# Weight products in unsplit fp32 on the column groups of the array, for a hybrid mLSTM and HGRN2 layer

## The chip, the cores and the metric

The kernel runs on one core of one Trainium2 chip. The core has a matrix engine (TensorE; PE in the profile, its weight loads PEld), a vector engine (VectorE, DVE), a scalar engine (ScalarE, ACT), a general engine (GpSimd, POOL) and an engine that only issues transfers (SyncE, SP). Data lie in an on-chip memory of 128 partitions (SBUF); TensorE writes to eight banks of a second memory (PSUM), from which VectorE and ScalarE take the results. The metric is the device time of the core in microseconds.

## The reference

One layer of a decoder trunk is applied to 320 tokens: a prompt of 256, and eight sequences of eight new tokens with a state each. Everything is in fp32.

```python
D_MODEL, D_FF = 2048, 8192

def layer(x, ...):
    proj = x @ w_in                                 # 2048 x 16392, cut into q, k, v, gates ...
    h, C, n, m = mlstm(q, k, v, ig, lf, C0, n0, m0)     # 4 heads, 256 x 512 state
    branch_a = layernorm(h) * ml_norm_g * sigmoid(ml_o)
    o, S = hgrn2(hq, log(f), 1 - f, hi, S0)             # 8 heads, 128 x 256 state
    branch_b = rms(o) * hg_norm_g * silu(hg_g)
    merged = sigmoid(gate_a) * (branch_a @ w_branch_a) + sigmoid(gate_b) * (branch_b @ w_branch_b)
    x1 = layernorm(ALPHA * x + merged @ w_out)
    hid = square(relu(x1 @ w_up))
    return layernorm(ALPHA * x1 + hid @ w_down), C, n, m, S
```

The outputs are the new rows and the new states of both mixers, for the prompt and for each of the eight sequences.

## The kernel before

**Layout.** Activations lie transposed: 16 blocks of 128 channels on the partitions, with the 320 tokens as columns. All weight matrices are cut into 304 tiles of 2048 inputs by 128 outputs (`tile_list`), taken in a fixed order: the mLSTM heads (v, k, q, with some merge gates between), the HGRN2 heads, the output gates, the two branch projections, the output projection, and four rounds of `up` and `dn` of 16 tiles each. A tile comes in two units of 1024 inputs, 512 KB each, and is summed over 16 steps of k in one PSUM bank. The first three tiles (`FIRST`) come with x itself and make up the lead.

**The product.** TensorE gets no plain fp32 operands in the weight loop. Each operand is split into a high part, rounded to the type `float32r`, and a low part, the rounded rest. A step of k is three matmuls of a 128 x 128 weight block and 128 x 320 tokens: high by high, high by low, low by high. In `run_main`:

```python
self.mm(o, hi[:, kk], mh[:, k, :], start=k == 0, stop=False)
self.mm(o, hi[:, kk], ml[:, k, :], start=False, stop=False)
self.mm(o, lo[:, kk], mh[:, k, :], start=False, stop=k == KT - 1)
s.t["pe"] = max(s.t["pe"], at) + 441.0
```

The weights are split on the chip: `prep` takes a unit out of one of three raw buffers `wr`, lets ScalarE write the high part (`wh`, in later stages a part of `bb`) and VectorE the low part (`wl` or `bb`), and then has the raw buffer loaded again (`reload`, on SP's queue). The operands x, the two branches, the merged branches, the normalised x1 and the hidden rows are split in the same way as they are made (`split`), into pairs such as `xh` and `xl`, `bah` and `bal`, `bbh` and `bbl`. The attention products of both mixers are partly split (numerator, final state, HGRN2 output, the sums over ones) and partly plain fp32 matmuls (scores, row sums).

**Small products on parts of the array.** Three kinds of matmul use only some columns or rows of the array: the projection for the two mLSTM gates at the end of `lead` (16 matmuls, L768 to L770), whose 32 outputs go to the four 32-wide column groups in turn; the product of the sample queries with their states (`m_sample`, `h_state`), eight matmuls of 32 outputs in a block; and the updates of the sample states (`m_adds`, `h_update`), four matmuls of 32 rows in a block. The first two are plain fp32.

**Order.** One Python program writes the instructions of all engines in the order of a plan. The class `Sched` keeps a planned time for each engine; `run_main` writes the steps of the weight loop one by one, and after each one `pump` lets the chains of small work (evacuations, the two mixers, LayerNorm, transfers) write what they can by the plan. The plan takes its durations from formulas: `pe_r` for a rounded matmul, `pe_f` for an fp32 one, `act` and `dve` for the other engines, 441 ns for a step of the weight loop. Each engine then runs its own instructions in that order and waits on semaphores; the plan's times themselves are not in the program. Transfers are issued by SP in one queue, some of them ("lazy") only when the plan has few bytes under way. Three PSUM banks serve the weight tiles, more from the output gates and the output projection on, and the others the small products.

**Ends.** After the last `dn` tile come the last LayerNorm, its scaling of all 16 blocks on VectorE and ScalarE with the stores of y, and, on TensorE between them, the final states of the prompt: `m_C` (16 products of 128 x 512 over three matmuls each) and `h_S` (16 fp32 matmuls of 128 x 256). Their operands were put into DRAM by the mixers (`kD`, `vD`, `sD`, `iD`).

Of the kernel before, what the change touches and what calls it, by code (L numbers as in the profile page):

```python
# [21 lines left out]
KT = 16  # L22
# [51 lines left out]
FIRST = 3  # L74
# [212 lines left out]
def pe_r(n):  # L287
    return max(108.0, n * 0.425)
# [44 lines left out]
class Program:  # L333
    def __init__(self, tc, nc, d, pools):
# [7 lines left out]
        self.xh2 = p.tile([128, KT, TOK + 2], F32R, name="xh", tag="xh")  # L342
        self.xl2 = p.tile([128, KT, TOK + 2], F32R, name="xl", tag="xl")
        self.xh, self.xl = self.xh2[:, :, 0:TOK], self.xl2[:, :, 0:TOK]
        self.RAW, self.HL = 3, 3
# [8 lines left out]
        self.ra = p.tile([128, 6656], F32R, name="ra", tag="ra")  # L354
# [21 lines left out]

    def dma(self, out, in_):
        self.nc.sync.dma_start(out, in_)
        self.s.transfer(self.s.t["sp"], 4 * math.prod(out.shape), 4 * min(run(out), run(in_)))


    def carve(self):
# [13 lines left out]
        A, B, C, R = Part(self.f1), Part(self.f2), Part(self.f3), Part(self.ra[:, 0:6400])  # L396
# [3 lines left out]
        self.vt = Pool([Part(self.f1, 4608).three(3, 512)])  # L400
# [3 lines left out]
        self.kw = Pool([B.three(2, 320)])  # L404
# [13 lines left out]
        self.shl = Pool([(R(384), R(384), R(256))])  # L418
        self.vhl = Pool([R(2048).rearrange("p (x s v) -> p x s v", x=2, s=2)])
        self.vs = Pool([R(512)])  # L420
        self.khl = Pool([R(1024).rearrange("p (x s k) -> p x s k", x=2, s=2)])
# [3 lines left out]
        A, B, R = Part(self.f1, 6144), Part(self.f2), Part(self.rh)  # L425
# [9 lines left out]
        self.hkz0 = self.ra[:, 5376:6400]  # L435
        self.phl = Pool([self.ra[:, 3776:5376].rearrange("p (x c) -> p x c", x=2)])
        self.hkst = Pool([self.hkz0[:, 0:256].rearrange("p (g k) -> p g k", g=2)])
# [11 lines left out]
    def carve_h(self):  # L449
# [7 lines left out]
        rxb = self.pool.tile([128, 4096], F32R, name="rxb", tag="rx")  # L457
        X, R, V, W, Z = self.Part(rxb), self.Part(self.ra), self.Part(self.ra), self.Part(rxb, 2880), self.Part(rxb, 3840)
        self.nc.gpsimd.memset(rxb[:, 3840:4096].bitcast(F32), 0.0)
        self.halves = Pool([(V(512), V(512), W(448), W(448))])  # L460
        self.vp = Pool([V(256), rxb[:, 2624:2880]])
        self.ats = Pool([(Z(128), Z(128))])
        self.bah = Slices([(X if j < 12 else R)(TOK) for j in range(KT)])
        self.bal = Slices([R(TOK) for _ in range(KT)])
# [13 lines left out]
    def carve_x(self):  # L478

        self.sx = []  # L480
        for name, n in (("xh", 6), ("xl", 2)):
            R = self.Part(self.pool.tile([128, KT * (TOK + 2)], F32, name=name + "s", tag=name))
            self.sx += [R(768) for _ in range(n)]

    def carve_o(self):
        R = self.Part(self.pool.tile([128, 4096], F32, name="oC", tag="rx"))
        self.oC = [R.three(2, 512) for _ in range(MH)]
        self.oS = self.Part(self.pool.tile([128, 6656], F32, name="oS", tag="ra")).three(HH, 256)

    def carve_b(self):  # L490

        self.bb = self.pool.tile([128, 10240], F32R, name="bb", tag="f1")
        R = self.Part(self.bb)
        self.bbh, self.bbl = R.three(KT, TOK), R.three(KT, TOK)
        R = self.Part(self.bb)
        wide = [R(2048) for _ in range(5)]
        self.wx = [(w[:, 0:1024], w[:, 1024:2048]) for w in wide]
        self.wxv = [w.rearrange("p (x s v) -> p x s v", x=2, s=2) for w in wide]


    def prep(self, must=False):

        u = self.next_prep
        if u >= len(UNITS) or not self.hl_free:
            return False
        now = self.s.t["pe"]
        if must:
            self.s.until(lambda: u in self.raw_at)
        elif u not in self.raw_at:
            return False  # L510
        if not must and (self.raw_at[u] > now + 200 or self.hl_free[0][0] > now + 200 or self.s.t["dve"] > now + 1200):
            return False
        at, buf = self.hl_free.pop(0)
        raw = self.wr[:, u % self.RAW, :]
        hi, lo = buf
        s = self.s
        e = s.use("act", max(at, self.raw_at[u]) + LAT, act(1048))
        self.A(hi, raw)
        e = s.use("dve", e + LAT, dve(1034))
        self.V().tensor_tensor(lo, raw, hi.bitcast(F32), ALU.subtract)  # L520
        self.unit[u] = (buf, e + LAT)
        self.next_prep += 1
        if u + self.RAW < len(UNITS):
            s.spawn(self.reload(u + self.RAW, e), -1)
        return True

    def reload(self, u, at):
        t = yield ("sp", 620, lambda: self.dma(self.wr[:, u % self.RAW, :], self.d["wt"][u]), (at,))
        self.raw_at[u] = t

    def run_main(self):
# [3 lines left out]
        for n in range(len(UNITS) * 8):  # L535
# [4 lines left out]
            if k == 0:  # L540
                self.before(i, t)
                mh, ml, evs = self.moving(t)
                todo[i] = self.take(), mh, ml, evs
            b, mh, ml, evs = todo[i]
            o = b[:, :mh.shape[2]]
            while self.prep(u not in self.unit):
                pass
            assert u in self.unit, (u, self.next_prep)
            (hi, lo), at = self.unit[u]
# [3 lines left out]
            kk = slice(128 * (k % 8), 128 * (k % 8) + 128)  # L553
            self.mm(o, hi[:, kk], mh[:, k, :], start=k == 0, stop=False)
            self.mm(o, hi[:, kk], ml[:, k, :], start=False, stop=False)
            self.mm(o, lo[:, kk], mh[:, k, :], start=False, stop=k == KT - 1)
            s.t["pe"] = max(s.t["pe"], at) + 441.0
            if k % 8 == 7:
                self.give(u)
# [4 lines left out]
        self.carve_o()  # L564
# [11 lines left out]
    def give(self, u):  # L576

        now, hl = self.s.t["pe"], self.unit[u][0]
        wide = any(hl is w for w in self.wx)
        rest = self.next_prep >= len(UNITS)  # L580
        if u + 16 < len(UNITS) or not (rest or (self.n_vx < 3 if wide else self.n_kx < 1)):
            self.hl_free.append((now, hl))
        elif wide:
            self.n_vx += 1
            self.vx.free.append((now, self.wxv[[hl is w for w in self.wx].index(True)]))
        else:
            self.n_kx += 1
            self.kx.free += [(now, x.rearrange("p (x s k) -> p x s k", x=2, s=2)) for x in hl]


    def moving(self, t):
        kind = t[0]
        if kind == "wa":
            return self.bah, self.bal, self.ba_ev
        if kind == "wb":
            return self.bbh, self.bbl, self.bb_ev
        if kind == "wo":
            return self.bah, self.bal, self.mg_ev
        if kind == "up":
            return (self.xh, self.xl, self.xs_ev) if t[2] else (self.xh2, self.xl2, self.zg_ev)  # L600
        if kind == "dn":
            return self.bah, self.bal, self.hid_ev[t[2]]
        return self.xh, self.xl, None

    def before(self, i, t):
# [29 lines left out]
        elif kind == "wo" and h == 0:  # L635
# [3 lines left out]
            self.hl_free += [(s.t["pe"], x) for x in self.wx[:4]]  # L639
            R = self.Part(self.wxv[4].rearrange("p x s v -> p (x s v)"))  # L640
            self.lns = [R.three(2, TOK) for _ in range(3)]
# [3 lines left out]
        elif kind == "dn" and c == 0 and h == 0:  # L645
            s.spawn(self.xs_(), 0)
        elif i == len(TILES) - 8:
# [10 lines left out]
    def start(self):  # L658
# [11 lines left out]
        self.unit, self.raw_at, self.next_prep = {}, {}, 0  # L670
# [12 lines left out]
        for u in range(self.RAW):  # L683
            self.dma(self.wr[:, u, :], d["wt"][u])
            self.raw_at[u] = 19000.0 + 1500.0 * u
        self.dma(self.cst, d["cst"])
        self.dma(self.f2[:, 448:704], d["spread"])
        self.spread = self.ra[:, 6400:6656].rearrange("p (g n) -> p g n", g=2)
# [7 lines left out]
        self.hl_free, self.gw = [], gw  # L696
        for e in s.t:
            s.t[e] = 2000.0
        s.wire, s.lands = 22000.0, [22000.0] * 8
# [24 lines left out]
    def lead(self):  # L724

        s, v = self.s, self.nc.vector
        f = lambda x: x.bitcast(F32)
        flat = lambda x: x.rearrange("p a b -> p (a b)")
        wh, wl = flat(self.wh), flat(self.wl)
# [4 lines left out]

        def halves(x, h, l, n, at):
            e = s.use("act", at + LAT, act(n))
            self.A(h, x)
# [1468 lines left out]
```

## Time and profile before

| | us |
|---|---|
| median of three runs | 2277.47 |
| lowest and highest of them | 2276.78, 2277.49 |
| span of the profiled execution, first to last instruction | 2275.6 |
| TensorE busy, in the profile | 2267.5 |
| VectorE busy | 1392.1 |
| ScalarE busy | 1170.8 |

The profile page has, from the top: busy time by engine; the span in 40 slices, with the granted clock of TensorE and the traffic; the transfer queues; the chain of work that ended last; the costliest groups of instructions, by source line, engine, operation and operands, with count, busy time, mean duration and the idle time before them; and the transfers. Because nearly every matmul is recorded by one helper, all have the line L375; ScalarE's have L369 and SP's transfers L378. In a row such as `bank<-xh,wl 128*128 128x320 f32`, the operands are followed by the rows and columns of the array that are used and by the shape of the streamed operand. Matmuls overlap in the pipeline and the profile's durations hold its depth, so the pace of a stream is read from starts, or from a stretch's length and its count, not from the duration of one.

### The profile page before, as it was taken

To read this page: it belongs to the slowest core of one execution; us is meant where nothing else is said; L and a number is where in the kernel's file an instruction comes from. 1 tells how busy PE (TensorE), PEld (TensorE's weight loads), DVE (VectorE), ACT (ScalarE), POOL (GpSimd) and SP (SyncE) were. 2 spreads that over 40 slices of the span, in tenths; PEclk is the share of its full clock that TensorE was granted. 3 is DMA by queue.
4 is the path that set the end of the run, shared out by engine and by line. 5 is a ranking of instruction groups with operands and counts; after the bars stand their busy time and mean duration, and the time that the engine had idled before them with its cause. 6 is when DMAs were issued, how large, how long until landed. Compare 5 with 4: busy or idle time off the path is not lost.

```text
span 2275.6 us, 39057 instructions
## 1 busy us (share of the span) xinstructions
PE 2267.5 (100%) x15518; PEld 2230.4 (98%) x15518; DVE 1392.1 (61%) x2426; ACT 1170.8 (51%) x2081; POOL 12.5 (1%) x36
## 2 busy tenths in 40 slices
PE   9999999999999999999999999999999999999998
PEld 9999999999999999999999999999999999999998
DVE  5676777777777777666555767544444444444456
ACT  6566555678777766444433446533432343234334
POOL 0000000000000000000000000000000000000000
PEclk9999999999999999999999999999999999999999
DMA  7588898666666575555556544444444444444476
GB/s 283 175 266 253 277 285 248 211 191 189 188 195 211 178 216 175 175 173 172 172 173 198 193 153 147 148 150 151 153 148 148 149 151 153 150 148 148 150 229 194
DMA packets 227438, 424.95 MB, mean 187 GB/s; under 512 B 96436, under 2 KB 122932, under 8 KB 226232
## 3 DMA queue, kind: packets, MB, share of 16 engines
q1 hardware_dynamic: 222376, 415.98, 56.9%
q0 software_dynamic: 4736, 6.29, 1.2%
q8 instruction: 121, 1.98, 0.4%
q14 instruction: 61, 0.50, 0.1%
q10 hardware_dynamic: 144, 0.20, 0.0%
HBM read 371.49 MB, written 50.90 MB: 186 GB/s over the span
## 4 chain that ended last, share of the span: by engine, by line
PE 97%; ACT 2%; DVE 0%; issue 0%; ACTq 0%; POOL 0%; DVEq 0%; POOLq 0%
PE bank L375 97%; ACT f L369 1%; ACT wh L369 0%; ACT f3m L369 0%; ACT ra L369 0%; ACT oC L369 0%; DVE f3m L2090 0%; DVE f3m L2097 0%; DVE wl L520 0%; ACT oS L369 0%; ACT xh L369 0%; ACTq L2202 0%; ACT f3h L369 0%; DVE f L1975 0%; DVE f L1974 0%
## 5 line engine op out<-in xcount | busy, mean ns | idle before, releaser
L520 DVE TENSOR_TENSOR wl<-wr,wh 128x1024 fp32r<-128x1024 f32 x440 | 538.8, 1225 | 432.3 <-ACT wh L369 429.2
L375 PE MATMUL bank<-xh,wh 128*128 128x320 f32 (+1 forms) x2504 | 786.5, 315 | 0.0
L375 PE MATMUL bank<-xh,wl 128*128 128x320 f32 (+1 forms) x2504 | 774.4, 310 | 0.0
L375 PE MATMUL bank<-xl,wh 128*128 128x320 f32 (+1 forms) x2504 | 772.1, 309 | 0.0
L369 ACT ACTIVATE wh<-wr 128x1024 fp32r<-128x1024 f32 x440 | 465.4, 1058 | 456.1 <-PE bank L375 437.0
L375 PEld LDWEIGHTS bank<-xh,wh 128*128 128x128 f32 x2504 | 471.2, 188 | 9.2 <-issue 7.3
L375 PEld LDWEIGHTS bank<-xl,wh 128*128 128x128 f32 x2504 | 471.3, 188 | 3.0
L375 PEld LDWEIGHTS bank<-xh,wl 128*128 128x128 f32 x2504 | 471.6, 188 | 0.2 <-DVE wl L520 0.2
L369 ACT ACTIVATE bb<-wr 128x1024 fp32r<-128x1024 f32 x162 | 171.6, 1059 | 296.0 <-PE bank L375 276.0
L520 DVE TENSOR_TENSOR bb<-wr,bb 128x1024 fp32r<-128x1024 f32 x162 | 198.5, 1225 | 195.2 <-ACT bb L369 195.0
L375 PE MATMUL bank<-ra,wh 128*128 128x320 f32 x1008 | 276.2, 309 | 0.7 <-DVE ra L1778 0.7
L375 PE MATMUL bank<-ra,bb 128*128 128x320 f32 x1096 | 255.5, 309 | 0.0
L375 PE MATMUL bank<-xh,bb 128*128 128x320 f32 (+1 forms) x1136 | 253.8, 309 | 0.0
L375 PE MATMUL bank<-rxb,bb 128*128 128x320 f32 x1088 | 249.1, 309 | 0.0
L375 PEld LDWEIGHTS bank<-xh,bb 128*128 128x128 f32 x1136 | 191.0, 188 | 0.0
L375 PE MATMUL bank<-rxb,wl 128*128 128x320 f32 x608 | 187.9, 309 | 0.0
L375 PE MATMUL bank<-rxb,wh 128*128 128x320 f32 x608 | 187.9, 309 | 0.0
L375 PEld LDWEIGHTS bank<-ra,bb 128*128 128x128 f32 x1096 | 185.2, 188 | 0.0
L375 PEld LDWEIGHTS bank<-rxb,bb 128*128 128x128 f32 x1088 | 184.6, 188 | 0.0
L375 PEld LDWEIGHTS bank<-ra,wh 128*128 128x128 f32 x1008 | 181.3, 188 | 0.9 <-DVE ra L1778 0.9
L375 PE MATMUL bank<-xl,bb 128*128 128x320 f32 (+1 forms) x568 | 175.5, 309 | 0.0
L369 ACT ACTIVATE f<-f 32x128 f32<-32x128 f32 (+6 forms) x405 | 150.7, 373 | 37.1 <-DVE f L1343 19.0
(274 smaller groups left out, 2257.3 us busy)
## 6 DMA issues: line engine op xcount, KB each, us to landing
wr<-wt SPq DMA_DIRECT2D x602, 512.0 KB, 3.4
rx<-C SPq DMA_DIRECT2D x36, 256.0 KB, 5.1
Cs<-rx SPq DMA_DIRECT2D x36, 256.0 KB, 4.5
f<-C SPq DMA_DIRECT2D x28, 256.0 KB, 4.7
Cs<-f SPq DMA_DIRECT2D x28, 256.0 KB, 5.5
f<-first SPq DMA_DIRECT2D x6, 704.0 KB, 9.6
vD<-ra SPq DMA_DIRECT2D x4, 1024.0 KB, 6.5
f<-S SPq DMA_DIRECT2D x8, 512.0 KB, 5.1
```

The source lines that it names most:

```text
L369: return self.nc.scalar.activation(out, in_, func, **kw)
L375: self.nc.tensor.matmul(*a, **kw)
L520: self.V().tensor_tensor(lo, raw, hi.bitcast(F32), ALU.subtract)
```

## The change

All weight products take plain fp32 operands, each as four matmuls of 32 outputs, one for each column group of the array, with the same streamed operand:

```diff
+    def mm4(self, out, w, x, start=True, stop=True, **kw):
+        for a in range(4):
+            c = slice(32 * a, 32 * a + 32)
+            self.nc.tensor.matmul(out[c], w[:, c], x, start=start, stop=stop, **kw)
...
-            (hi, lo), at = self.unit[u]
+            s.until(lambda: u in self.unit)
+            w, at = self.unit[u]
...
-            kk = slice(128 * (k % 8), 128 * (k % 8) + 128)
-            self.mm(o, hi[:, kk], mh[:, k, :], start=k == 0, stop=False)
-            self.mm(o, hi[:, kk], ml[:, k, :], start=False, stop=False)
-            self.mm(o, lo[:, kk], mh[:, k, :], start=False, stop=k == KT - 1)
-            s.t["pe"] = max(s.t["pe"], at) + 441.0
+            self.mm4(b[:, :x.shape[2]], w[:, 128 * (k % 8):128 * (k % 8) + 128], x[:, k, :], k == 0, k == KT - 1)
+            s.t["pe"] = max(s.t["pe"], at) + pe_4(x.shape[2])
```

The splits of weights and operands go, and with them `prep`, `reload` and `split`. The operands are written once, in fp32, into `x`, `ba` and `bb`. The room of the halves goes to raw weight buffers: ten from the start (`RAW`), four more once `bb` is laid out; `give` has a freed buffer loaded with the next unit at once.

```diff
-FIRST = 3
+FIRST, RAW = 3, 10
...
 def pe_r(n):
-    return max(108.0, n * 0.425)
+    return max(108.0, n * 0.425) + 120.0
+
+
+def pe_4(n):
+    return max(60.0, n * 0.84)
...
-        self.xh2 = p.tile([128, KT, TOK + 2], F32R, name="xh", tag="xh")
-        self.xl2 = p.tile([128, KT, TOK + 2], F32R, name="xl", tag="xl")
...
-        self.wr = p.tile([128, self.RAW, 1024], F32, name="wr")
-        self.wh = p.tile([128, self.HL, 1024], F32R, name="wh")
-        self.wl = p.tile([128, self.HL, 1024], F32R, name="wl")
+        self.x2 = p.tile([128, KT, TOK + 2], F32, name="x", tag="x")
+        self.x = self.x2[:, :, 0:TOK]
+        self.ba = p.tile([128, KT, TOK], F32, name="ba")
+        self.wr = p.tile([128, RAW, 1024], F32, name="wr")
...
+    def load(self, u, buf, at):
+        t = yield ("sp", 620, lambda: self.dma(buf, self.d["wt"][u]), (at,))
+        self.unit[u] = (buf, t)
```

`pe_4` is the plan's time for the four matmuls of an `mm4` together; it replaces the 441 ns of a step and `pe_f`. The same `mm4` takes the place of the split products of the mixers, of the plain fp32 products on the whole array, and of the sums over ones in LayerNorm and in HGRN2. The mLSTM numerator and the LayerNorm totals:

```diff
-                for x, w in ((sh, vh), (sh, vl), (sl, vh)):
-                    st, sp = n == 0, n == 3 * len(jobs) - 1
-                    yield ("pe", pe_r(512), lambda: self.mm(b, x[:, c:c + 128], w[:, s, :], start=st, stop=sp))
-                    n += 1
+            for n, (c, s) in enumerate(jobs):
+                yield ("pe", pe_4(512), lambda: self.mm4(b, E[:, c:c + 128], vt[:, s, :], n == 0, n == len(jobs) - 1))
...
-        yield from self.split(x, hi, lo)
-        for i, y in enumerate((hi, lo)):
-            yield ("pe", 147, lambda: self.mm(p[:, :TOK], self.ones.bitcast(F32R), y, start=i == 0, stop=stop and i == 1))
+        yield ("pe", pe_4(TOK), lambda: self.mm4(p[:, :TOK], self.ones, x, start, stop))
```

The spread of the sample rows and the row-tiled updates of the sample states stay as rounded products, each with its split. `kD` and `vD` hold fp32 instead of two halves, are half as large, and are loaded by SP during the second `up` round (`m_load`) instead of by POOL near the end.

More of the change, by code (lines that the diff above doesn't have):

```diff
@@ L456, in carve_h @@
             self.nc.gpsimd.memset(x, 0.0)
[L457 to L464, printed above, removed]
+        X = self.Part(self.pool.tile([128, 4096], F32, name="rxh", tag="rx"))
+        ats = [X(128) for _ in range(2)]
+        for x in ats:
+            self.nc.gpsimd.memset(x, 0.0)
+        self.ats = Pool(ats)
+        self.pb.free.append((self.s.t["pe"], X(800)))
         now = self.s.t["pe"]
@@ L480, in carve_x, with carve_b @@
         self.sx = []
-        for name, n in (("xh", 6), ("xl", 2)):
-            R = self.Part(self.pool.tile([128, KT * (TOK + 2)], F32, name=name + "s", tag=name))
+        for tag, size, n in (("x", KT * (TOK + 2), 6), ("fv", 2176, 2)):
+            R = self.Part(self.pool.tile([128, size], F32, name=tag + "s", tag=tag))
             self.sx += [R(768) for _ in range(n)]
-    def carve_o(self):
+    def carve_b(self):
+        bb = self.pool.tile([128, 10240], F32, name="bb", tag="f1")
+        self.bb = self.Part(bb).three(KT, TOK)
+        self.give([bb[:, lo:lo + 1024] for lo in range(6144, 10240, 1024)])
+        R = self.Part(bb)
+        self.ck = [(R(512), R.three(2, 512)) for _ in range(MH)]
@@ L501, in prep @@
[L501 to L525, printed above, removed]
@@ L541, in run_main @@
                 self.before(i, t)
[L542 to L548, printed above, removed]
-            (hi, lo), at = self.unit[u]
+                x, evs = self.moving(t)
+                todo[i] = self.take(), x, evs
+            b, x, evs = todo[i]
+            s.until(lambda: u in self.unit)
+            w, at = self.unit[u]
+            at += LAT
             if evs is not None:
@@ L574, in take @@
         return b
[L576 to L588, printed above, removed]
     def moving(self, t):
@@ L646, in before @@
             s.spawn(self.xs_(), 0)
+        elif kind == "up" and c == 1 and h == 0:
+            self.ck_ev = [Ev() for _ in range(MH)]
+            for j in range(MH):
+                s.spawn(self.m_load(j), 3)
         elif i == len(TILES) - 8:
@@ L682, in start @@
         self.dma(self.vec, d["vec"])
-        for u in range(self.RAW):
+        for u in range(RAW):
             self.dma(self.wr[:, u, :], d["wt"][u])
[L685 to L688, printed above, removed]
+            self.unit[u] = self.wr[:, u, :], 19000.0 + 1300.0 * u
+            if u == 1:
+                self.dma(self.cst, d["cst"])
+                self.dma(self.f2[:, 448:704], d["spread"])
         nc.gpsimd.memset(self.eps, EPS)
@@ L817, in rows @@
         p1 = yield acq(self.sbank)
-        yield ("pe", pe_f(T), lambda: self.mm(p1[:, :T], sel, gs, start=True, stop=True))
+        yield ("pe", pe_4(T), lambda: self.mm4(p1[:, :T], sel, gs))
         yield rel(self.sbank, b)
@@ L1251, in m_sample @@
         yield rel(self.bc, bc)
-        yield wait(m["KS"])
+        yield wait(m["KS"], m["CP"])
         yield post(m["end"])
@@ L1684, in h_S @@
         b = yield acq(self.mbank)
-        yield ("pe", 2 * pe_f(256), lambda: [self.mm(
-            b[:, 0:256], x[:, 128 * i:128 * i + 128], x[:, 256 + 256 * i:512 + 256 * i], start=i == 0, stop=i == 1) for i in range(2)])
+        yield ("pe", 2 * pe_4(256), lambda: [self.mm4(
+            b[:, 0:256], x[:, 128 * i:128 * i + 128], x[:, 256 + 256 * i:512 + 256 * i], i == 0, i == 1) for i in range(2)])
         self.s.spawn(self.S_out(h, b), 0, self.s.t["pe"])
```

315 lines of the change are left out of this document (104 added, 211 removed).

## The prediction

> **What bounds the kernel now.** I read the head of the page first, then its chain of waits, then the view of stretches for two long pure stretches of the weight loop.
>
> ```profile
> span 2275.6 us, 39057 instructions
> PE 2267.5 (100%) x15518; PEld 2230.4 (98%) x15518; DVE 1392.1 (61%) x2426; ACT 1170.8 (51%) x2081; POOL 12.5 (1%) x36
> PEclk9999999999999999999999999999999999999999
> PE 97%; ACT 2%; DVE 0%; issue 0%; ACTq 0%; POOL 0%; DVEq 0%; POOLq 0%
> 1100.00:1466.00 366.00, 366.00 (x2487) 365.74 (x2487) 232.60 (x344) 172.57 (x252) 0.00 (x0) 1.00 0.52 171
> 1700.00:2250.00 550.00, 550.00 (x3754) 550.00 (x3753) 256.90 (x312) 194.06 (x233) 5.34 (x7) 1.00 0.49 156
> ```
>
> TensorE is busy at full clock for the whole span, the chain that ended last is TensorE for 97%, and the DMA engines are busy 52% and 49% in the two stretches (the number before the last). So the time is the sum of the matmuls, and nothing else needs a price until that sum falls. The last two rows give the unit of the sum: 550 us for 3754 matmuls is 0.1465 us each, 366 for 2487 (some evacuation products among them) 0.1472. A step of k in the weight loop is three of these (high by high, high by low, low by high), so 0.4395 to 0.4415 us; I take 0.440. There are 304 tiles of 16 steps, 4864 steps, 48 of them in the lead.
>
> **What the change puts in its place** is in the trace of before already. The gate projection at the end of `lead` (L768 to L770) is 16 unsplit fp32 matmuls of 128 rows, 32 outputs and 320 tokens, written to the four column groups in turn: the very shape and order of `mm4`. These are the PE rows of the timeline around it, then two groups of the page and of the view by line and shape.
>
> ```profile
> 26.96 0.31 PE L375 MATMUL bank<-xh,wl 128*128 128x320 f32 x1
> 27.19 1.82 PE L375 MATMUL bank<-f,f 128*32 128x320 f32 x24
> 28.83 0.72 PE L375 MATMUL bank<-f 128*32 128x320 f32 x8
> 29.48 0.42 PE L375 MATMUL bank<-xh,wh 128*128 128x320 f32 x1
> 27.49 0.72 PE L375 MATMUL bank<-f,f 128*32 128x320 f32 x8
> 27.19:29.37 2.18, 2.18 (x33) 0.94 (x32) 0.65 (x1) 2.18 (x4) 0.20 (x1) 1.00 0.00 0
> L375 PE MATMUL bank<-ones 128*128 128x128 f32 x18 | 4.2, 430 | 1.0 <-POOL ones L666 1.0
> L375 PE MATMUL bank<-rx,f 128*32 128x512 f32 x72 | 13.6, 599 | 0.0
> L375 PE MATMUL bank<-f 128*32 128x512 f32 x56 | 12.6, 597 | 0.0
> L375 PE MATMUL bank<-ra 128*128 128x512 f32 x52 | 20.2, 395 | 0.0
> ```
>
> Count first. Sixteen calls left 24 + 8 = 32 records; the 64 sample products on column groups left 72 + 56 = 128; the nine warm-up matmuls of ones left 18; the 52 rounded products of this width (9 and 2 and 2 for each of four heads) left 52. An fp32 matmul is two instructions on the array, a rounded one is one. Then the pace. The 32 records run in eight rounds, the four groups of a round side by side (a narrow window at 27.9 shows 8 records from 27.49 on, two rounds overlapping). The second round starts at 27.49 and the seventh at 28.83: five rounds in 1.34 us, 0.268 each; with the first, which follows the change of tile shape, six in 1.64, 0.273. The whole block is 2.18 us for four steps of four, 0.545. I take 0.269 a round, nearer to the undisturbed ones. The four groups do share the time of one, but each of them has two rounds to run, so a step of `mm4` at 320 columns is 2 x 0.269 = **0.538 us, against 0.440** for the three rounded products.
>
> **The sum.** Weight loop: 4864 x (0.538 - 0.440) = +477 us. With the ends of the rows, 0.536 - 0.4415 to 0.546 - 0.4395, it is +460 to +518.
>
> The smaller products. Two widths have rows, from the last stretch of the timeline and from the sample block of a head:
>
> ```profile
> 2260.43 0.84 PE L375 MATMUL bank<-bb,wh 128*128 128x512 f32 x3
> 2261.11 1.52 PE L375 MATMUL bank<-bb,wl 128*128 128x512 f32 x6
> 2262.48 5.34 PE L375 MATMUL bank<-xhs 128*128 128x256 f32 x24
> 104.98 1.48 PE L375 MATMUL bank<-f 128*32 128x512 f32 x10
> 106.30 0.60 PE L375 MATMUL bank<-f 128*32 128x512 f32 x2
> 106.84 0.50 PE L375 MATMUL bank<-ra 32*128 32x512 f32 x4
> ```
>
> Nine rounded products of 512 take 2.05 us, 0.228 each. Column-group rounds of 512 start at 104.98 and, three rounds later, at 106.30: 0.44, the first one again the long one; I use 0.43, so 0.86 for a group of four. Between 320 and 512 I read both on a straight line (an estimate): 256 costs 0.119 rounded and 0.43 for a group, 480 costs 0.214 and 0.81. Then: 12 products of the mLSTM numerator and 16 of its final state, three rounded for one group, 28 x (0.86 - 0.68) = 5; the sample numerator, 4 x (0.86 - 0.46) = 2; the lag sums over ones, 8 x (0.81 + 0.54 - 0.43 - 0.29) = 5; the HGRN output, 8 x (1.29 - 1.07) + 8 x (0.43 - 0.24) = 3; six LayerNorm totals, 6 x (0.54 - 0.29) = 2. Together +17 us. Of this, the 16 final-state products (3 us) lie behind the last tile, where the rows above show TensorE dense from product to product, so they count too. The scores and other products that were fp32 on the whole array already (0.55 us at 320 columns, below) keep their time: bounds 0 to +30 for all of this.
>
> Changes of tile shape. The waits view has the price of all of them now:
>
> ```profile
> PEld bank L375 <- issue: 24.1, 79, 0.8
> L520 DVE TENSOR_TENSOR wl<-wr,wh 128x1024 fp32r<-128x1024 f32 x440 | 538.8, 1225 | 432.3 <-ACT wh L369 429.2
> L369 ACT ACTIVATE wh<-wr 128x1024 fp32r<-128x1024 f32 x440 | 465.4, 1058 | 456.1 <-PE bank L375 437.0
> L375 PEld LDWEIGHTS bank<-xl,wh 128*128 128x128 f32 x2504 | 471.3, 188 | 3.0
> wr<-wt SPq DMA_DIRECT2D x602, 512.0 KB, 3.4
> ```
>
> 79 gaps, 24.1 us. The blocks on column groups (one gate block, eight for mLSTM samples, eight for HGRN) cease to be changes; the row-tiled state products (16 and 8 blocks) still are, and the twelve to sixteen spread blocks and the transposes, which stay on the whole array, become ones. About as many as before: 0, bounds -24 to +24.
>
> What is taken from VectorE and ScalarE (all 602 unit splits; the two rows above are 440 of them, the others write `bb`) is off the path: both engines waited for TensorE or for each other over 430 us in just these groups. It hides behind the matmuls now and its removal buys nothing; the plain copies that remain are shorter than what they replace. The 602 weight loads on SP's queue are the same ones, now into ten, later fourteen, buffers; a unit lasts eight steps, 4.3 us instead of 3.5, against 3.4 us from issue to landing, so the transfers move from half busy to less. The wait of the loop changes its object: a unit's first matmul waits for the landing of its transfer instead of VectorE's low half. All of TensorE stands behind such a wait, but ten units are loaded ahead, 43 us of work. The eight reloads for the final mLSTM state go from POOL's queue to SP's, at the second `up` block, half as large as now and long before they are needed. The program order was made with a faster TensorE in mind (`pe_4` counts 0.84 ns a column, one round where the rows show two). An engine that is slower than its plan finds its inputs ready; what waits is ACT's and VectorE's evacuations, which have 8.6 us a tile. I price it at nothing. LDWEIGHTS of 32 columns sit inside the rounds in the block above (32 in 0.94 us of 2.18), so they add nothing either.
>
> The lead. It starts without the split, so about 1 us sooner, and one of its early waits for the splits goes too; it stays TensorE-bound since three groups are 1.6 us a step: -2, bounds -4 to +3.
>
> Sum against the profiled execution: 2275.6 + 477 + 17 - 2 = 2767.6. The median of the runs shown, 2277.47, is 1.9 above that span, so **2769.5 us**. All ends added, 2277.5 + 460 - 24 - 4 = 2709.5 and 2277.5 + 518 + 30 + 24 + 3 = 2852.5; they will not all fall one way, and 2715 to 2850 is the forecast's own range.
>
> **Rivals.**
>
> One round instead of two (faster). If the array got through a group's fp32 product in a single round of 0.269, as `pe_4` assumes, a step would cost 0.269 and the loop would lose 4864 x 0.171 = 832 us: TensorE 2277 - 832 - some 20 for the small products that shorten too, 1430. Then the transfers take over:
>
> ```profile
> q1 hardware_dynamic: 222376, 415.98, 56.9%
> GB/s 283 175 266 253 277 285 248 211 191 189 188 195 211 178 216 175 175 173 172 172 173 198 193 153 147 148 150 151 153 148 148 149 151 153 150 148 148 150 229 194
> ```
>
> 416 MB at the best slice, 285 GB/s, are 1460 us, so about 1500. It decides from a step under 0.440. For it speaks only that four groups start within one round; against it the count, two records to a call, in all 16 calls here and all 64 sample products. The Trainium skill, TensorEngine Tiling (Array Packing), section Theoretical Speedup, gives up to four-fold where a dimension is 32 or less; set against the 0.55 us of a whole-array fp32 product, that would be 0.14 us a step. The rows bear it out only for four 32-wide products against one 32-wide product, not against a 128-wide one. 8%.
>
> Instruction supply (slower still). A step becomes 8 matmuls and 8 weight loads instead of 3 and 3. From 33.6 ns an instruction on (0.538 / 16) the sequencer would set the pace. The block above issued 64 in 2.18 us, 34 ns each, without a gap, and the next one started after the usual pause; but no longer run of this density is in the trace, and the loop itself shows only that 73 ns each is sustained (550 us for 7507). So the price lies between nothing and 16 x 73 = 1.17 us a step, +3070 us on the forecast, 5840. I take nothing, as the dense block is the nearest row. The Trainium skill, TensorE: Matmul & The Clock Gate, Part 2, step 2, says that with hardware decode off a MATMUL costs the sequencer about 62 ns. By it alone eight take 0.50 us, still under 0.538; with the loads at the same price a step is 0.99 us and the time near 4970. No row here tells which decode is on. 7%.
>
> The four do not run side by side, but as one whole-array fp32 product:
>
> ```profile
> 2251.15 0.71 PE L375 MATMUL bank<-f3m,ones 128*128 128x320 f32 x2
> 2251.70 0.72 PE L375 MATMUL bank<-f,ones 128*128 128x320 f32 x2
> ```
>
> 0.55 us a step, +58 on the forecast, 2830: it is inside the range, and I count it there, with 3%.
>
> **Chances and range.** The forecast with its own range has 80%, the whole-array case 3%, one round 8%, supply 7%, and 2% stay for what I do not see (half of them near no change). About 0.2% is what a measurement of this kernel can tell from no change. Faster: 8%. Same: 1%. Slower: 91%. The range 2715 to 2850 holds 83%; neither far case has to be reached.
>
> **What would show it.** Right: in the page after, PE still 99% or more of the span and near 97% of the chain; some 39,000 matmul records of 128*32 with 320 columns; in a stretch of the loop eight matmuls every 0.538 us; the DMA share below 0.45 there; VectorE's and ScalarE's busy time down by more than 600 us each. Wrong on the fast side: four records to a step, a DMA share near 0.9. Wrong on the supply side: weight loads with idle time before them put down to issue, and rounds further apart than 0.27 us. Wrong on my zero for the order: PE idle behind evacuations at the tile borders.

## The result, and the profile after

| | us | ratio to before |
|---|---|---|
| before, median of 4 runs | 2277.36 | |
| after, median of 4 runs (2803.37 to 2804.77) | 2804.15 | 1.2313 (95%: 1.2296 to 1.2331) |
| forecast | 2769.5 (2715 to 2850) | |

The kernel became 526.8 us slower. The sign, the rough size and the range were right; the forecast was 34.7 us too low. The page of after, head, slices and chain:

```profile
span 2801.9 us, 87737 instructions
PE 2772.6 (99%) x41048; PEld 1587.7 (57%) x41048; DVE 585.6 (21%) x1584; ACT 473.3 (17%) x1281; POOL 7.6 (0%) x31
PE   9999999889999999999999999999999999999998
PEclk9999999989999999999999999999999999999999
PE 98%; ACT 1%; DVE 1%; DMA 0%; issue 0%; ACTq 0%; POOL 0%; DVEq 0%; POOLq 0%
...
wr<-wt SPq DMA_DIRECT2D x494, 512.0 KB, 3.4
```

VectorE lost 806.5 us of work and ScalarE 697.5, and neither is seen in the time: TensorE is busy 99% of the span and 98% of the chain. But the eighth and the ninth slice show 8 for TensorE, and the ninth shows 8 for its clock, where before had nines. The view of stretches of after, first that region as a whole, then the part of it that is starved, then two pure stretches of the weight loop (busy us of PE, weight loads, VectorE, ScalarE, GpSimd; granted clock; DMA share; GB/s):

```profile
500.00:800.00 300.00, 280.41 (x4078) 131.44 (x4074) 125.41 (x413) 131.84 (x427) 3.23 (x11) 0.95 0.54 165
546.10:585.30 39.20, 21.52 (x122) 5.78 (x112) 23.40 (x62) 17.65 (x48) 0.00 (x0) 0.74 0.46 141
1100.00:1466.00 366.00, 366.00 (x5442) 251.58 (x5436) 64.75 (x156) 28.73 (x54) 0.00 (x0) 1.00 0.45 148
2000.00:2400.00 400.00, 400.00 (x5948) 240.06 (x5942) 23.00 (x47) 12.24 (x26) 0.00 (x0) 1.00 0.38 124
```

The last row is the step: 400 us for 5948 matmuls, eight to a step, 0.538 us, the forecast's figure to the third digit. The second row is what the forecast did not have: 39 us in which TensorE ran 122 matmuls, against some 580 in such a time in the loop. TensorE's timeline there, with its idle time and what ended it in brackets:

```profile
539.75 6.38 PE L382 MATMUL bank<-x,wr 128*32 128x320 f32 x92
545.94 0.35 PE L382 MATMUL bank<-misc,f 128*32 128x1 f32 x24
556.09 0.79 PE L377 MATMUL bank<-ra 128*128 128x512 f32 x1 [9.80 <-DVE ra L911]
556.81 1.94 PE L382 MATMUL bank<-fv,f 128*32 128x512 f32 x8
...
567.24 3.64 PE L382 MATMUL bank<-fv,f 128*32 128x512 f32 x16 [1.80 <-DVE rx L1209]
...
574.67 1.89 PE L377 MATMUL bank<-rx,f 128*32 128x512 f32 x4 [1.45 <-DMA rx<-C]
...
576.92 1.07 PE L382 MATMUL bank<-fv,f 128*32 128x512 f32 x8
...
583.09 2.23 PE L377 MATMUL bank<-ra 32*128 32x512 f32 x3 [2.28 <-DVE f L1209]
585.25 5.04 PE L382 MATMUL bank<-x,wr 128*32 128x320 f32 x44
```

The rows that multiply by a weight buffer, `bank<-x,wr`, stop at 546 and come back at 585.25. Between them stands nothing but the last mLSTM head's small products, one behind the other, with waits for VectorE, for ScalarE and, in one row, for a transfer. In the longest gap, 9.8 us, ScalarE writes that head's values block by block. This is ScalarE's timeline of after:

```profile
549.95 4.24 ACT L371 ACTIVATE fv<-f 32x256 f32<-32x256 f32 x11
```

To see where the difference lies, I added up the starts of all matmul records: the lead up to the first step behind the gate block, the steps of the weight loop (from a step's record to the next record), the blocks of other matmuls between them, and the tail from the last weight record to the end of the span. What lies between a step and a block beside it is counted in the record that comes first. Two experiments told of below are in the table too (the slower plan, and whole-array products in the loop).

| us | before | after | slower plan | whole-array loop |
|---|---|---|---|---|
| lead | 29.5 | 33.3 | 33.7 | 34.0 |
| weight steps | 2138.9 | 2603.0 | 2599.0 | 2629.9 |
| blocks between | 81.8 | 134.8 | 104.1 | 157.9 |
| tail | 25.4 | 30.8 | 25.9 | 30.9 |
| span | 2275.6 | 2801.9 | 2762.7 | 2852.7 |

### The profile page after: what moved, and what is told of

It is laid out like the page before. It is cut to its first block, busy times and chain, and to the rows that moved or that the text cites. A ratio compares the mean times of both kernels' runs of the same rounds, so it can differ in the third digit from the quotient of the medians.

```text
span 2801.9 us, 87737 instructions
## 1 busy us (share of the span) xinstructions
PE 2772.6 (99%) x41048; PEld 1587.7 (57%) x41048; DVE 585.6 (21%) x1584; ACT 473.3 (17%) x1281; POOL 7.6 (0%) x31
## 3 DMA queue, kind: packets, MB, share of 16 engines
q1 hardware_dynamic: 216872, 415.98, 46.6%
## 4 chain that ended last, share of the span: by engine, by line
PE 98%; ACT 1%; DVE 1%; DMA 0%; issue 0%; ACTq 0%; POOL 0%; DVEq 0%; POOLq 0%
PE bank L382 97%; PE bank L377 2%; ACT f L371 0%; ACT fv L371 0%; ACT ra L371 0%; DMA Cs<-f 0%; DVE f3m L1958 0%; DMA hH<-f 0%; ACT f3m L371 0%; DVE f3m L1951 0%; DVE oS L1588 0%; DVE f L1209 0%; DVE f L1023 0%; DVE f L989 0%; ACT misc L371 0%
## 5 line engine op out<-in xcount | busy, mean ns | idle before, releaser
L382 PE MATMUL bank<-x,wr 128*32 128x320 f32 (+1 forms) x21248 | 1474.0, 433 | 0.0
L382 PEld LDWEIGHTS bank<-x,wr 128*32 128x32 f32 x21248 | 761.9, 109 | 639.0 <-issue 39.4
L382 PE MATMUL bank<-ba,wr 128*32 128x320 f32 x8960 | 609.7, 432 | 0.0
L382 PEld LDWEIGHTS bank<-ba,wr 128*32 128x32 f32 x8960 | 376.7, 110 | 226.2
L382 PE MATMUL bank<-ba,bb 128*32 128x320 f32 x3328 | 227.8, 432 | 0.0
L382 PE MATMUL bank<-x,bb 128*32 128x320 f32 (+1 forms) x2944 | 201.7, 432 | 0.0
L382 PEld LDWEIGHTS bank<-ba,bb 128*32 128x32 f32 x3328 | 140.7, 110 | 83.3
L382 PEld LDWEIGHTS bank<-x,bb 128*32 128x32 f32 x2944 | 124.2, 109 | 74.3 <-issue 2.0
L382 PE MATMUL bank<-bb,wr 128*32 128x320 f32 x1408 | 95.5, 432 | 0.0
L371 ACT ACTIVATE f<-f,misc 128x320 f32<-128x320 f32 x162 | 90.8, 560 | 18.1 <-DVE f L1916 10.2
L382 PEld LDWEIGHTS bank<-bb,wr 128*32 128x32 f32 x1408 | 67.2, 110 | 27.6
L382 PE MATMUL bank<-bb 128*32 128x320 f32 (+1 forms) x768 | 57.9, 459 | 0.0
L382 PEld LDWEIGHTS bank<-bb 128*32 128x32 f32 x768 | 34.6, 110 | 21.6 <-issue 8.6
L382 PE MATMUL bank<-f 128*32 128x320 f32 (+4 forms) x768 | 43.8, 345 | 0.0
```

What stands on the lines that cost most here:

```text
L371: return self.nc.scalar.activation(out, in_, func, **kw)
L382: self.nc.tensor.matmul(out[c], w[:, c], x, start=start, stop=stop, **kw)
```

## The experiments

Theory: a step costs 2 rounds of 0.269 us, the four groups side by side, and the missing 35 us come from the order that the plan wrote with half of TensorE's real time. Rivals: the missing time lies in the column groups themselves or in changes of tile shape; and the two far rivals of the prediction, one round and instruction supply.

**A plan with TensorE's real time.** `pe_4` and the gate block are doubled in the plan. The work of the engines stays the same, only its order changes.

```diff
-    return max(60.0, n * 0.84)
+    return max(120.0, n * 1.68)
...
-        s.t["pe"] += 1100.0
+        s.t["pe"] += 2200.0
```

> The changed kernel, with the plan told what the loop takes: pe_4 1.68 ns a column with a floor of 120 instead of 0.84 and 60, 2200 instead of 1100 for the gate block. The instructions are the same, only their order differs. In the changed kernel's trace TensorE lacks weight steps from 546.1 to 585.3 us, a stretch of 39 us with some 10 us of small products in it. Theory A: the order was made for a TensorE of half the pace, whose plan ran out of weight steps at the first HGRN2 tiles; a right plan puts weight steps between the last mLSTM products, the stretch closes, and the time is 2804 - 29 = 2775 (2765 to 2785). Rival: the last mLSTM head ends late because of its new buffers and chains, whatever the plan; then the stretch stays and the time is 2798 to 2810.

Measured: 2765.15 us (2764.70 to 2765.59, 4 runs), 1.2141 of before (1.2123 to 1.2159), 39.0 us less than after. The head of its page and its stretches:

```profile
span 2762.7 us, 87781 instructions
PE 2758.0 (100%) x41048; PEld 1632.1 (59%) x41048; DVE 608.2 (22%) x1584; ACT 475.6 (17%) x1281; POOL 7.6 (0%) x31
```

```profile
500.00:800.00 300.00, 300.00 (x4628) 146.94 (x4624) 123.98 (x383) 124.35 (x405) 1.82 (x5) 1.00 0.51 162
1000.00:2700.00 1700.00, 1700.00 (x25240) 1112.64 (x25236) 223.48 (x497) 120.94 (x255) 0.00 (x0) 1.00 0.40 134
```

The same 41,048 matmuls, and the stretch from 500 to 800 us has 300 busy of 300, where after had 280. The timeline of this kernel's TensorE shows how: at the same time it is already at the small products of an HGRN2 head, and weight steps stand between them.

```profile
548.27 0.40 PE L382 MATMUL bank<-f,f3h 128*32 128x128 f32 x8
548.49 0.72 PE L382 MATMUL bank<-x,wr 128*32 128x320 f32 x8
549.03 1.05 PE L377 MATMUL bank<-f3h 128*32 128x256 f32 x16
549.89 1.80 PE L382 MATMUL bank<-x,wr 128*32 128x320 f32 x24
```

By the table, 30.7 of the 39 us are in the blocks between, 4.9 in the tail, 4.0 in the steps, less 0.4 in the lead. I had expected about 29 us, the starved stretch alone; the tail was not in that figure. Its reading, from the last TensorE row of either kernel, first of after, then of the slower plan:

```profile
2791.32 1.90 PE L382 MATMUL bank<-fvs 128*32 128x256 f32 x32
```

```profile
2756.98 1.96 PE L382 MATMUL bank<-fvs 128*32 128x256 f32 x32
```

TensorE ends 8.7 us before the span does in after (2801.9 - 2793.2), and 3.8 us before it with the slower plan: there the last LayerNorm's scaling is done by the time the final states are, in after VectorE and ScalarE still have it to do. Three pieces of after's chain of waits in order of time (start, us, what), L1588 taking out a final state, the others scaling:

```profile
2790.79 0.42 DVE oS L1588
...
2796.22 0.41 DVE f3m L1958
...
2796.66 1.74 ACT f3m L371 x3
```

**Which of the two numbers.** The formula alone, the gate block left as it was:

```diff
-    return max(60.0, n * 0.84)
+    return max(120.0, n * 1.68)
```

> After with pe_4 doubled in the plan, the gate block left at 1100 ns. Theory A (the order made with half of TensorE's time loses the 39 us, and pe_4 is what carries it): 2764 to 2769 us. Theory B (the block at the end of the lead, 1.1 us too short in the plan, shifts the order enough to bring the starved stretch): near 2800.

Measured: 2765.01 us in one run, span 2762.5. All of it is `pe_4`; the gate block's number in the plan changes nothing that the time shows.

**One column group.** In steps 1 to 14 of each tile only the first group of 32 outputs is multiplied; outputs 32 to 127 of a tile get 2 of their 16 steps.

```diff
-            self.mm4(b[:, :x.shape[2]], w[:, 128 * (k % 8):128 * (k % 8) + 128], x[:, k, :], k == 0, k == KT - 1)
+            xk, wk = x[:, k, :], w[:, 128 * (k % 8):128 * (k % 8) + 128]
+            if 0 < k < KT - 1:
+                self.mm(b[0:32, :x.shape[2]], wk[:, 0:32], xk, start=False, stop=False)
+            else:
+                self.mm4(b[:, :x.shape[2]], wk, xk, k == 0, k == KT - 1)
```

> The changed kernel with only the first of the four column groups issued in steps 1 to 14 of each tile behind the lead (outputs 32 to 127 of a tile then hold two steps of sixteen). Theory A: the four groups run side by side and each needs two rounds of 0.269 of its own, so three quarters of the matmuls can go without any gain: 2795 to 2806. Rival: the pace of a step is that of issuing or of the groups one after the other; then a step falls to a quarter, 0.135 us, TensorE to some 1100 us and the transfers set the time at about 1500.

Measured: 2801.67 us in one run, 2.5 us under after. A stretch of the loop, and a piece of TensorE's timeline (L377 is the single group, L382 the four):

```profile
2000.00:2400.00 400.00, 400.00 (x2052) 166.67 (x2045) 23.03 (x47) 12.20 (x26) 0.00 (x0) 1.00 0.37 123
```

```profile
2156.36 7.43 PE L377 MATMUL bank<-ba,wr 128*32 128x320 f32 x27
2163.37 0.47 PE L382 MATMUL bank<-ba,wr 128*32 128x320 f32 x3
2163.63 0.43 PE L377 MATMUL bank<-ba,wr 128*32 128x320 f32 x1
```

A tile has 14 x 2 + 2 x 8 = 44 records here; 2052 records are 46.6 tiles in 400 us, 8.58 us a tile, 0.536 a step. In the second fence 27 matmuls of the single group start at 2156.36 and its next at 2163.63: 7.27 / 27 = 0.269 apart. So one group alone takes as long as four, and the other three ran beside it: three quarters of the matmuls gone, nothing gained. One round a step is out, and so is any limit by the number of instructions, which is a third here.

**Fewer columns, the same instructions.** Steps 1 to 14 stream only 128 of the 320 tokens; tokens 128 to 319 get 2 of the 16 steps. The count of instructions stays.

```diff
-            self.mm4(b[:, :x.shape[2]], w[:, 128 * (k % 8):128 * (k % 8) + 128], x[:, k, :], k == 0, k == KT - 1)
+            n = 128 if 0 < k < KT - 1 else x.shape[2]
+            self.mm4(b[:, :n], w[:, 128 * (k % 8):128 * (k % 8) + 128], x[:, k, :n], k == 0, k == KT - 1)
```

> The changed kernel with 128 instead of 320 streamed columns in steps 1 to 14 of each tile behind the lead (tokens 128 to 319 get two steps of sixteen). It asks how dense the instructions may be. Theory A: the round goes with the columns, 128 / 320 of 0.267 plus 2.5 ns, 0.109; a step is 0.218, an instruction 13.6 ns, a tile 4.1 us; TensorE 304 tiles 1260 and all else 150 to 190, the transfers at 254 GB/s near their best, so 1450 to 1650 with steps of 0.218 within a unit. Rival: the sequencer supplies one instruction in 20 ns or more (the densest 256 in the changed kernel's trace took 25.9 each); then a step is 0.32 to 0.41 us and the time 1700 to 2150.

Measured: 1635.03 us in one run. A stretch, a piece of TensorE's timeline, and a row of the waits:

```profile
1200.00:1600.00 400.00, 379.39 (x11477) 349.65 (x11472) 65.89 (x139) 27.70 (x59) 0.00 (x0) 1.00 0.71 231
```

```profile
1287.09 4.34 PE L382 MATMUL bank<-ba,wr 128*32 128x128 f32 x128 [0.20 <-issue]
1291.91 4.34 PE L382 MATMUL bank<-ba,wr 128*32 128x128 f32 x127 [0.48 <-issue]
```

```profile
PE bank L382 <- issue: 126.4, 160, 2.9
```

Over 400 us TensorE was given 22,949 instructions, one in 17.4 ns, pauses included. After needs one in 33.6. So supply does not bind after. Between the pauses a step of 128 columns has a median of 0.218 us from start to start, as expected, which is 13.6 ns an instruction. At this density, over twice that of after, pauses show that the profile puts down to issue (in brackets above), 126 us in all. In the stretch shown they come after 127 or 128 matmul records, or about a multiple of that; why, the runs do not show.

**Whole-array products in the loop.** One fp32 matmul of 128 outputs instead of four of 32, in the weight loop behind the lead; the small products stay on column groups.

```diff
-            self.mm4(b[:, :x.shape[2]], w[:, 128 * (k % 8):128 * (k % 8) + 128], x[:, k, :], k == 0, k == KT - 1)
+            self.mm(b[:, :x.shape[2]], w[:, 128 * (k % 8):128 * (k % 8) + 128], x[:, k, :], start=k == 0, stop=k == KT - 1)
```

> The changed kernel with one fp32 matmul of 128 outputs instead of four of 32 in the 4816 steps of the weight loop behind the lead. Theory A: an fp32 product is two passes of two cycles a column on whatever columns it uses, so the four groups together do what the whole array does: a step of 0.538 to 0.55 us (0.55 in the two last LayerNorm totals of before) instead of 0.538, 2804 + 0 to 58, so 2800 to 2865. Rival: the column groups do gain against the whole array, by the factor of two that pe_4 against pe_f says; then a step is 1.08 us and the time near 5400.

Measured: 2853.95 us (2852.94 to 2854.74, 4 runs), 1.2530 of before (1.2509 to 1.2551), 49.8 us more than after. A stretch of its loop:

```profile
2000.00:2400.00 400.00, 400.00 (x1487) 281.06 (x1487) 23.06 (x47) 14.63 (x31) 0.00 (x0) 1.00 0.38 129
```

1487 records are 0.269 each, two to a step, 0.538 again; the rival of a much slower whole-array product falls. So the extra 49.8 us are not in the step. The 26.9 us that the table has more for weight steps than after lie in the first and last steps beside the blocks: the steps between those take 2397.2 us in either kernel. What is dearer are the ways into and out of the small products: TensorE's timeline of this kernel, then of after, around the same work, a score product of 256 columns and two steps of the loop:

```profile
206.23 0.64 PE L382 MATMUL bank<-f 128*32 128x256 f32 x8
206.79 1.34 PE L377 MATMUL bank<-x,wr 128*128 128x320 f32 x4
208.07 0.64 PE L382 MATMUL bank<-f 128*32 128x256 f32 x8
```

```profile
200.46 0.61 PE L382 MATMUL bank<-f 128*32 128x256 f32 x8
200.89 1.26 PE L382 MATMUL bank<-x,wr 128*32 128x320 f32 x16
201.97 0.61 PE L382 MATMUL bank<-f 128*32 128x256 f32 x8
```

From product to product 1.84 us with a change of tile shape in and out, 1.51 without: 0.33 us for one detour. Both traces have 203 blocks between, in the same order, so each can be set against its counterpart, with the step before and the step behind it. The 161 blocks whose products run on column groups alone are detours here and none in after: each costs 0.335 us more at the median, 58 us together. The 17 blocks on the whole array alone are detours in after and none here: each costs 0.33 us less. The other 25 differ by 2 us together. Whether the difference goes when the shapes agree got its own run.

**Whole-array products everywhere, with the slower plan.** `mm4` itself becomes one matmul, so that the loop and most small products have one tile shape again (the gate block and the sample products stay on column groups, the updates of the sample states on row groups). The plan is the slower one:

```diff
     def mm4(self, out, w, x, start=True, stop=True, **kw):
-        for a in range(4):
-            c = slice(32 * a, 32 * a + 32)
-            self.nc.tensor.matmul(out[c], w[:, c], x, start=start, stop=stop, **kw)
+        self.mm(out, w, x, start=start, stop=stop, **kw)
```

> The kernel with the slower plan, but every group of four (weight loop, attention products, sums over ones) is one fp32 matmul on the whole array. Theory A (a whole-array fp32 product has the same 0.538 us a step, and the +49.8 us of the run with whole-array products in the loop alone came from the changes of tile shape around the small products): those changes are gone, so the time is that of the slower plan, 2765 us, or a little less: 2752 to 2772. Theory B (the +49.8 us belong to the whole-array product itself, for instance to its weight loads of 128 columns): about 2765 + 50 = 2815, 2805 to 2830.

Measured: 2767.99 us (2766.72 to 2768.30, 4 runs), 1.2154 of before (1.2134 to 1.2175). Its page and a stretch:

```profile
span 2765.7 us, 26902 instructions
PE 2760.1 (100%) x10610; PEld 1925.9 (70%) x10610; DVE 607.7 (22%) x1584; ACT 475.0 (17%) x1281; POOL 7.6 (0%) x31
```

```profile
1000.00:2700.00 1700.00, 1700.00 (x6313) 1195.78 (x6312) 223.52 (x497) 120.74 (x255) 0.00 (x0) 1.00 0.40 133
```

About a quarter of the matmuls, 10,610 instead of 41,048, and the time is that of the four groups with the same plan, within 2.8 us (0.1%). So the 49.8 us were the mix of shapes, and for fp32 products of this size the cut into four groups buys nothing against one product of 128 outputs. Set block against block as above, the 139 blocks that went from column groups to the whole array with the loop differ by 0.005 us at the median; eight sample blocks that stayed on column groups became detours, at 0.34 us each. The small remainder of 2.8 us is not traced further.

**Two products instead of three, in the kernel before.** In steps 1 to 14 of each tile behind the lead, the product of the weights' high part with the operands' low part is left out (4214 matmuls); the splits are still made.

```diff
-            self.mm(o, hi[:, kk], ml[:, k, :], start=False, stop=False)
+            if not 0 < k < KT - 1:
+                self.mm(o, hi[:, kk], ml[:, k, :], start=False, stop=False)
```

> The kernel before without the product of the weights' high part and the operands' low part in steps 1 to 14 of every tile behind the lead (301 x 14 = 4214 matmuls left out); the splits are still made. Theory A (the kernel before is bound by its count of rounded products, 0.1465 us each): 2277.4 - 617 = 1660 us, up to 1760 where VectorE's splits, now at about 84 per cent, come late. Theory B (a step's 0.440 us is set by something beside the products, such as the splits or the weight loads): over 2000 us.

Measured: 1897.58 us in one run, between the two theories and outside both. Stretches of its early, middle and late part:

```profile
200.00:400.00 200.00, 176.05 (x1069) 154.71 (x1069) 152.51 (x300) 122.11 (x233) 1.68 (x6) 0.94 0.89 276
600.00:800.00 200.00, 169.13 (x1085) 156.75 (x1084) 154.62 (x381) 152.06 (x374) 0.73 (x2) 0.94 0.64 195
1600.00:1800.00 200.00, 200.00 (x1362) 200.00 (x1361) 126.91 (x145) 102.39 (x122) 0.00 (x0) 1.00 0.66 211
```

In the last stage (`up` and `dn`) 1362 matmuls fill 200 us, 0.147 each, as before: there a step is its products and nothing else, and a product left out is 0.147 us gained. In the two stretches of the mixers' stages TensorE is idle 12 to 15% of the time, its granted clock is 0.94, and TensorE has only 29% of the chain on the page. So TensorE did bind the kernel before, as the prediction read it; but in the first half the other engines were close behind, and a TensorE with up to a third less to do met them (in the first stretch the transfers, too, are busy 89%). The change went the other way, and they never came up.

## Why the prediction was right, and where it was not

**Two rounds of 0.269: right.** The forecast took the pace of the loop from 32 records at the end of the lead of before. The loop has it over 400 us (0.538 a step), the single group has it too, and so has the whole array. The 4816 steps behind the lead were priced at 4816 x 0.098 = +472; by the table they cost +460 with the slower plan and +464 in after. The table's steps hold what lies between them and the small blocks: they took 2138.9 / 4816 = 0.4441 us in before, not 0.440, and 0.5397 with the slower plan, not 0.538. So the ways into and out of blocks made 20 us on the side of before and 8 on the other.

**Small products: +17, of it 3 in the tail.** The blocks between cost +22.3 with the slower plan, inside the bounds of 0 to +30. In after they cost +53.0, most of the rest being the starved stretch. The tail, priced at +3, cost +0.5 with the slower plan and +5.4 in after.

**Changes of tile shape: 0, bounds ±24.** The waits on issue, the view that priced them, for after:

```profile
PEld bank L382 <- issue: 54.1, 252, 0.7
PEld bank L377 <- issue: 28.5, 54, 1.7
```

82.6 us in 306 gaps, against 24.1 in 79; with the slower plan the same two rows add up to 52.1 in 160. The count was wrong: there are twice as many such gaps with the slower plan, and more in after, where the starved stretch adds its own. The cost does not stand beside the terms above but inside them (the way into and out of a block), so the sum hardly noticed: steps and blocks together, +482 with the slower plan against +486 forecast. That is in part luck: the two terms missed in opposite directions, by -12 and +8.

**The lead: -2.** With its 48 steps at +0.098 that is +2.7; the first step behind it came 3.8 us later in after. Right within its bounds.

**What went from VectorE and ScalarE, and the loads: nothing. Right.** 1504 us of work gone in all, no gain; the unit loads still land in 3.4 us, and the DMA share is 0.38 to 0.45 in the pure stretches of the loop.

**The order: the step that failed.** The prediction said: "An engine that is slower than its plan finds its inputs ready; what waits is ACT's and VectorE's evacuations, which have 8.6 us a tile. I price it at nothing." The first half is true of a wait whose two ends are fixed. But the plan also chooses what stands next to what in TensorE's order. It believed in steps of 0.269 us, so in the plan the weight steps ran ahead of ScalarE and VectorE, until the next tile needed a set of buffers of the mixers (`s.until(lambda: self.hs.free)` in `before`). Weight steps stop in after behind tile 57 and come back with tile 58 (counted from 0 in `tile_list`), `hf` of the third HGRN2 head, a tile that asks for such a set; in before and with the slower plan the records on either side of the same border start no more than 0.25 us apart. Until that set was free the plan could write only the last mLSTM head's small work, and that work is a chain over three engines and the transfers. On the chip TensorE took twice as long for those steps, and ScalarE and VectorE waited for its results meanwhile; when they could begin on the last head, the steps that should have lain beside its chain had been spent. That is argued from the code and the timelines; what is shown, by changing one formula, is that the order costs 39.0 us and that the starved stretch goes with it. The forecast's own miss, 34.7 us, is these 39.0 less the 4.4 by which all other terms together came out too high. That the range held all the same is luck in this point: no bound in it stood for the order, and the room came from the bounds of the other terms. The prediction had even named the sign to look for, TensorE idle behind the other engines, and put it at the tile borders; it came at one tile of the HGRN2 heads, behind a chain of the other mixer.

**The rivals.** One round: out, by the single group. Supply: out, by 17.4 ns an instruction sustained, pauses included. The whole-array case: it was priced by a step of 0.55 us, taken from two lone pairs of records; the step is 0.538, and what made it dearer in the run was the change of shape. That the four groups take as long as one whole-array product is, at this size, shown: both are 0.538.

With the slower plan the kernel stands 4.4 us under the forecast and 487.7 us over before. No version of the fp32 products tried here comes near the three rounded ones, 0.440 a step. Rounded products on column groups were not tried.

## What to carry to other kernels

Count array rounds, not matmuls: here four 32-wide fp32 products side by side replaced one 128-wide product and took as long as it does, and one 32-wide product alone took as long as the four. A short block of the same shape and order in the old trace gave the pace of the whole new loop here. Where a planner writes the order, correct its durations together with the instructions: a plan that was wrong by two cost 39 us here, by the account above because it used up early the work that should have covered another chain.

## What the runs showed of the hardware

- An fp32 product of 320 columns takes 0.538 us on the whole array and on four column groups alike, as two records of 0.269; a rounded one takes 0.1465, so the fp32 product costs 3.7 rounded ones. The Trainium skill, FP8 and Floating Point Precision, section TensorE Precision Notes, counts four passes through the array for true fp32; by that, an estimate, 4 x 0.1465 = 0.586 us. The measured step is 8% less.
- The four groups do not stay in step. In the lead of after the four matmuls of a round start 3 to 4 ns apart (20.072, 20.076, 20.079, 20.082); at 2100 us one round starts at 0.042, 0.053, 0.054 and 0.096 us, the next at 0.312, 0.322, 0.323 and 0.365. Each keeps its own 0.269.
- A detour to another tile shape and back cost 0.33 us beside fp32 products of 320 columns, 0.335 at the median of 161 blocks. The Trainium skill, TensorEngine Tiling (Array Packing), section Key Properties, says that a change of tiling mode drains the array; the two timelines above fit that; they show the price of a detour, not the drain itself.
- TensorE's granted clock was lower where it paused: 0.74 in the 39 us of after with gaps up to 9.8 us, 0.94 in the two stretches of the kernel with two products where it was busy 85 to 88%. In the 39 us eight records of one kind, `bank<-fv,f` of 512 columns, took 1.94 us from 556.81 on, where the granted clock was 0.50, and 1.07 us from 576.92 on, where it was 1.00. A starved stretch so costs more than its idle time.
